# Putting two steps of a chunked scan inside an ordering block that names a matrix product

## The chip, the cores and the metric

The kernel runs on one core of one Trainium2 chip. A core has a matrix engine (PE in the profile, with its weight loads as PEld), three engines for elementwise work (DVE, ACT and POOL) and SP, which here only issues transfers. Every engine works off its own queue of instructions in the order in which they stand in it. The metric is the device time of one execution in microseconds (us).

## What is computed

One layer of a hybrid trunk over 384 rows of 2048 channels (256 rows of a new stream, and 8 running streams with 16 rows each). What matters here is the middle of it, a chunked state-space scan with 8 groups of 8 heads of 64 channels. In the reference one chunk goes so:

```python
cum = jnp.cumsum(dtc * A, axis=1)
decay = jnp.exp(jnp.where(causal, cum[:, :, None] - cum[:, None, :], -jnp.inf))
cb = jnp.einsum('btgn,bsgn->btsg', Cc, Bc)
xdt = xc * dtc[..., None]
y = jnp.einsum('btsgr,bsgrp->btgrp', cb[..., None] * decay, xdt)
y = y + jnp.einsum('btgn,bgrpn->btgrp', Cc, h) * jnp.exp(cum)[..., None]
w_end = jnp.exp(cum[:, -1][:, None] - cum)
h = h * jnp.exp(cum[:, -1])[..., None, None] + jnp.einsum('bsgn,bsgr,bsgrp->bgrpn', Bc, w_end, xdt)
```

Before it stand a normalisation and one large projection with a causal convolution, behind it a gated normalisation, two output projections and a squared-ReLU MLP. All of it is in 32-bit floats.

## The kernel before

**Large products.** Every weight tile of 128 x 1024 numbers is fetched by SP into a tile `w`, and `wsplit` (lines 66 to 72) splits it: ACT rounds it into a high part `wh` (line 70), DVE takes the difference as a low part `wl` (line 71). Three matrix products then stand for one: high by high, high by low, low by high (lines 98 to 100). PE therefore waits for ACT and DVE whenever a split is late. In the names of the profile `wl_z` is the low part of a weight tile for a z projection, `pj_z` the tile in the accumulation memory that the product goes to.

**The scan's blocks.** The loop over `g` from line 866 runs eight blocks, one for each group, and a short tail. Each block has ten projections (four for x, one each for B and C, four for z) and two pairs of heads. Between the projections stand the scan's short products, all queued on PE in a fixed row: `t_pp`, `t_cb`, `t_yT`, `t_Y`, `t_yi` and, in `state`, `t_su`. Around them lie the two steps that the change touches:

- `bside` (line 706): ACT rounds the transposed B of the block into its high part (line 708), DVE makes the low part (line 709), and nine small transfers on SP follow.
- `xside` (line 733), once for each pair: four products on DVE (line 738), two of them scaled copies `xdt` and two that scale the transposed x, `xT`, in place. Then `yis` (line 745, DVE, from the result of `t_yi`), the split of `xT` into `xhl` (lines 752 and 753), and ten small transfers on SP. `mside` follows in the first half of a block and makes `cbm` from `cb` on DVE (line 731).

The transposed x and B come from two transfers through main memory on the queue of POOL (lines 617 and 623), whose landing the steps wait for.

**What sets the order.** The kernel's functions are recorded line by line, and a scheduler of the library sets the order on each engine by what is ready first. The helper `behind` (line 56) ties the order where the kernel wants it:

```python
    def behind(ins):
        return nullcontext() if ins is None else tc.issue_after(ins.ins)
```

The library's `issue_after(ins)` adds an edge of issue order, without a wait for the end of `ins`, from each instruction that the block records *on the engine of `ins`*. Instructions of other engines in the block get none. `last[0]` is always the latest product on PE: `half`, `moving` and `lump` set it. `later` (line 75) is the other use of the helper, with `cut[0]`, a rounding on ACT, and `cut[1]`, a difference on DVE.

Of the kernel before, what the change touches and what calls it, by code (L numbers as in the profile page):

```python
# [6 lines left out]
F32 = mybir.dt.float32  # L7
F32R = mybir.dt.float32r
I32 = mybir.dt.int32
AF = mybir.ActivationFunctionType  # L10
ALU = mybir.AluOpType
# [3 lines left out]
P = 128  # L15
# [18 lines left out]
def build(ctx, tc, io):  # L34
    nc = tc.nc
    v, s, te, gp, sy = nc.vector, nc.scalar, nc.tensor, nc.gpsimd, nc.sync
# [16 lines left out]
    def sstile(name):  # L53
        return pss.tile([P, 512], F32, tag="ss", name=name)

    def behind(ins):
        return nullcontext() if ins is None else tc.issue_after(ins.ins)
# [44 lines left out]
    last = [None]  # L102
# [75 lines left out]
    def three(name):  # L178
        return [sstile(f"{name}_{b}") for b in range(3)]
# [180 lines left out]
    tok = small.tile([P, 11, NH], F32, name="tok")  # L360
    decb = small.tile([P, NH, NB], F32, name="decb")
    with tc.tile_pool(name="phc", bufs=1, reuse_waits="tile") as pc, tc.tile_pool(name="phc2", bufs=2, reuse_waits="tile") as pc2:
# [3 lines left out]
        for i in range(2):  # L366
            b = pc.tile([P, 640], F32, name=f"pbuf{i}")[:, :519]
# [190 lines left out]
    with tc.tile_pool(name="phd", bufs=2, reuse_waits="tile") as pd, tc.tile_pool(  # L558
# [5 lines left out]
        for i in range(3):  # L564
            b = pd1.tile([P, 24, 19], F32, name=f"cbuf{i}")
# [139 lines left out]

        def bside(D):
            bh, bl = (D.Bhl[:, a].rearrange("p b n -> p (b n)") for a in range(2))
            s.activation(bh, bl.bitcast(F32), AF.Copy)
            v.tensor_tensor(bl, bl.bitcast(F32), bh.bitcast(F32), ALU.subtract)
            bscr = b_scr[D.g]  # L710
            sy.dma_start(bscr, D.Bhl[:, :, 2, :].bitcast(F32))
            D.bs = bst[D.g % 2]
            for p4 in range(4):
                for h2 in range(2):
                    sy.dma_start(
                        D.bs[h2 * 64 + p4 * 16 : h2 * 64 + p4 * 16 + 16].bitcast(F32),
                        bscr.rearrange("(q h r) l n -> h l r q n", q=4, h=2)[h2, p4 // 2],
                    )
# [13 lines left out]

        def xside(S):
            S.xdt = pd.tile([P, 2, 3, P], F32, tag="xdt", name=f"xdt{S.nm}")
            for q in range(2):
                tv = S.xT[:, q].rearrange("p b (h q) -> p b h q", h=2)
                for o, i in ((S.xdt, 3), (S.xT, 6)):
                    v.tensor_tensor(
                        o[:, q].rearrange("p b (h q) -> p b h q", h=2),
                        tv,  # L740
                        tok[:, i : i + 3, S.h0 + q * 2 : S.h0 + q * 2 + 2].unsqueeze(3).to_broadcast([P, 3, 2, 64]),
                        ALU.mult,
                    )
            S.yis = pd.tile([P, 2, P], F32, tag="yis", name=f"yis{S.nm}", bufs=1)
            v.tensor_tensor(
                S.yis.rearrange("p j (h q) -> p (j h) q", h=2),
                S.yi.rearrange("p (h q) -> p h q", h=4),
                tok[:, 10, S.h0 : S.h0 + 4].unsqueeze(2).to_broadcast([P, 4, 64]),
                ALU.mult,
            )  # L750
            S.xhl = pd.tile([P, 2, 2, 3, P], F32R, tag="xhl", name=f"xhl{S.nm}", bufs=1)
            s.activation(S.xhl[:, 0], S.xT, AF.Copy)
            v.tensor_tensor(S.xhl[:, 1], S.xT, S.xhl[:, 0].bitcast(F32), ALU.subtract)
            xscr = x_scr[S.qd]
            for l in range(2):
                sy.dma_start(xscr[:, l], S.xhl[:, l, :, 2, :].bitcast(F32))
            S.xst = pd.tile([P, 4, 2 * P], F32R, tag="xst", name=f"xst{S.nm}", bufs=1)
            for p4 in range(4):
                for h2 in range(2):
                    sy.dma_start(  # L760
                        S.xst[h2 * 64 + p4 * 16 : h2 * 64 + p4 * 16 + 16].bitcast(F32),
                        xscr.rearrange("(q h r) l j n -> h l r q (j n)", q=4, h=2)[h2, p4 % 2],
                    )
# [102 lines left out]
        for g in range(G + 1):  # L866
# [37 lines left out]
            S = D.p[0]  # L904
            S.py = mmtile(f"py{S.nm}")
            if g:
                lump(lambda: t_pp(prev.p[1], S.py))
            lump(lambda: t_cb(D))
            bside(D)
            if g:  # L910
                lump(lambda: t_yT(prev.p[1]))
                lump(lambda: t_Y(prev.p[1]))
            lump(lambda: t_yi(S))
            xside(S)
            mside(D)
            if g:
# [30 lines left out]
            lump(lambda: t_Y(S))  # L947
            lump(lambda: t_yi(S1))
            xside(S1)
            state(S)  # L950
            final(S)
# [21 lines left out]
    with ExitStack() as phe:  # L973
# [21 lines left out]
        for nb in range(4):  # L995
# [4 lines left out]
            o = three(f"pj_sp{nb}")  # L1000
# [44 lines left out]
    with tc.tile_pool(name="phf", bufs=1, side="right", reuse_waits="tile") as pf, tc.tile_pool(  # L1045
# [80 lines left out]
        for nb in range(4):  # L1126
# [3 lines left out]
            o = [sstile(f"wo{nb}_{b}") for b in range(3)]  # L1130
# [156 lines left out]
    with tc.tile_pool(name="phg", bufs=1, reuse_waits="tile") as pg, tc.tile_pool(  # L1287
# [9 lines left out]
        for c8 in range(NC):  # L1297
            hh = []
            for f8 in range(8):
# [8 lines left out]
                h = pg2.tile([P, T], F32R, tag=f"hh{f8}", name=f"hh{f}", bufs=1)  # L1308
# [4 lines left out]
            for nb in range(4):  # L1313
                o = [sstile(f"wd{c8}_{nb}_{b}") for b in range(3)]
# [158 lines left out]
```

## Time and profile before

| | |
|---|---|
| median of three runs | 2702.86 us (2700.16, 2703.67, 2702.86) |
| the profiled execution | 2702.03 us |
| its span, first to last instruction | 2700.1 us |
| mean granted clock of the matrix engine | 0.993 |
| the eight blocks of the scan | from about 440 to 1220 us of the span |
| PE busy | 2647.5 us, 98% of the span |
| DVE, ACT, POOL busy | 1524.7, 1150.1, 245.2 us |

A row of waits names the engine and line that sat idle, what released it, the total in us, how often, and the longest. A row of the timeline has the start, the duration, the engine, the line, and in square brackets the idle time just ahead of it with its releaser. A row of the windows has, for each engine, the busy time and the count of instructions in that stretch, then the granted clock of PE, the share of the transfer engines and their rate.

### The profile page before, as it was taken

Reading aid. Unit: us, or ns where it says so; the run is one execution under the profiler, and the core shown is the slowest. Engines: PE = TensorE matmul, PEld = TensorE weight load, DVE = VectorE, ACT = ScalarE, POOL = GpSimd, SP = SyncE. Lnnn points to the kernel's source line nnn. Section 1 sums busy time; section 2 is a strip of 40 time slices with the busy share of each in tenths; the row PEclk is TensorE's granted clock in tenths of the full one; section 3 lists DMA queues with packets and bytes.
Section 4 is the critical chain, followed back from the end, with each engine's and each line's share of the span. In section 5 each row is a group of like instructions: output and inputs, shape, how many; then the busy total and the mean of one; then the engine's idle time right before and its main releaser. Section 6 shows DMA issues by size and latency. Waiting matters only on the chain.

```text
span 2700.1 us, 38584 instructions
## 1 busy us (share of the span) xinstructions
PE 2647.5 (98%) x15149; PEld 2463.7 (91%) x15149; DVE 1524.7 (56%) x2148; ACT 1150.1 (43%) x1806; POOL 245.2 (9%) x366
## 2 busy tenths in 40 slices
PE   9999999899999899999999999999999999999998
PEld 9998889898999899988888888989999999999897
DVE  6585336687787787866433345634444444444446
ACT  6443235456565565644422234633233333333233
POOL 0000002223223223311000000000000000000000
PEclk9999999999999999999999999999999999999999
DMA  7444446666666676766644454333334444444443
GB/s 269 152 132 157 145 151 210 201 222 224 228 228 221 207 249 209 226 205 225 230 156 156 156 187 156 125 133 135 138 133 137 137 133 136 138 133 138 135 133 132
DMA packets 153845, 467.10 MB, mean 173 GB/s; under 512 B 21120, under 2 KB 48320, under 8 KB 148672
## 3 DMA queue, kind: packets, MB, share of 16 engines
q1 hardware_dynamic: 134400, 389.90, 44.1%
q0 software_dynamic: 19264, 74.74, 8.0%
q8 instruction: 119, 1.95, 0.3%
q14 instruction: 62, 0.51, 0.1%
HBM read 414.97 MB, written 49.58 MB: 172 GB/s over the span
## 4 chain that ended last, share of the span: by engine, by line
PE 55%; DVE 2%; DMA 1%; issue 1%; ACT 0%; POOL 0%; DVEq 0%; POOLq 0%; ACTq 0%
PE pj_up L98 6%; PE pj_up L100 6%; PE pj_up L99 6%; PE wd L151 6%; PE wd L150 6%; PE wd L149 6%; PE pj_sp L149 3%; PE pj_sp L150 3%; PE pj_sp L151 3%; PE wo L151 2%; PE wo L150 2%; PE pj_gb L149 2%; PE wo L149 2%; PE pj_gb L151 2%; PE pj_gb L150 2%
## 5 line engine op out<-in xcount | busy, mean ns | idle before, releaser
L98 PE MATMUL pj_up<-x1h,wh_up 128*128 128x384 f32 (+1 forms) x1024 | 333.7, 326 | 0.0
L99 PE MATMUL pj_up<-x1l,wh_up 128*128 128x384 f32 (+1 forms) x1024 | 333.4, 326 | 0.0
L100 PE MATMUL pj_up<-x1h,wl_up 128*128 128x384 f32 (+1 forms) x1024 | 333.4, 326 | 0.0
L71 DVE TENSOR_TENSOR wl_wd<-w_wd,wh_wd 128x1024 fp32r<-128x1024 f32 x126 | 154.3, 1225 | 240.5 <-ACT wh_wd L70 240.5
L149 PE MATMUL wd<-wh_wd,hh 128*128 128x512 f32 x756 | 286.5, 379 | 0.0
L150 PE MATMUL wd<-wl_wd,hh 128*128 128x512 f32 x756 | 286.5, 379 | 0.0
L151 PE MATMUL wd<-wh_wd,hl 128*128 128x512 f32 x756 | 286.5, 379 | 0.0
L70 ACT ACTIVATE wh_wd<-w_wd 128x1024 fp32r<-128x1024 f32 x126 | 133.1, 1057 | 322.3 <-PE wd L151 261.9
L98 PE MATMUL pj_x<-xgh,wh_x 128*128 128x384 f32 x768 | 256.1, 333 | 2.6 <-DVE zs L929 2.6
L70 ACT ACTIVATE wh_up<-w_up 128x1024 fp32r<-128x1024 f32 x126 | 133.1, 1057 | 291.8 <-PE pj_up L99 231.8
L100 PE MATMUL pj_x<-xgh,wl_x 128*128 128x384 f32 x768 | 254.3, 331 | 1.0 <-DVE wl_x L71 1.0
L71 DVE TENSOR_TENSOR wl_up<-w_up,wh_up 128x1024 fp32r<-128x1024 f32 x126 | 154.3, 1225 | 177.9 <-ACT wh_up L70 177.7
L99 PE MATMUL pj_x<-xgl,wh_x 128*128 128x384 f32 x768 | 254.2, 331 | 0.0
L99 PEld LDWEIGHTS pj_up<-x1l,wh_up 128*128 128x128 f32 x1024 | 193.6, 189 | 0.2
L98 PEld LDWEIGHTS pj_up<-x1h,wh_up 128*128 128x128 f32 x1024 | 193.6, 189 | 0.2
L100 PEld LDWEIGHTS pj_up<-x1h,wl_up 128*128 128x128 f32 x1024 | 193.6, 189 | 0.0
L100 PE MATMUL pj_z<-xgh,wl_z 128*128 128x384 f32 x512 | 168.4, 329 | 12.6 <-DVE wl_z L71 12.5
L98 PE MATMUL pj_z<-xgh,wh_z 128*128 128x384 f32 x512 | 167.6, 327 | 0.8 <-ACT wh_z L70 0.8
L99 PE MATMUL pj_z<-xgl,wh_z 128*128 128x384 f32 x512 | 167.5, 327 | 0.0
L71 DVE TENSOR_TENSOR wl_sp<-w_sp,wh_sp 128x1024 fp32r<-128x1024 f32 x64 | 78.4, 1225 | 154.0 <-ACT wh_sp L70 154.0
L151 PEld LDWEIGHTS wd<-wh_wd,hl 128*128 128x128 f32 x756 | 142.9, 189 | 20.3
L149 PEld LDWEIGHTS wd<-wh_wd,hh 128*128 128x128 f32 x756 | 142.9, 189 | 20.1
(333 smaller groups left out, 5979.7 us busy)
## 6 DMA issues: line engine op xcount, KB each, us to landing
w_up<-w_up SPq DMA_DIRECT2D x128, 512.0 KB, 3.3
w_wd<-w_down SPq DMA_DIRECT2D x128, 512.0 KB, 3.3
w_x<-w_in SPq DMA_DIRECT2D x96, 512.0 KB, 4.5
w_z<-w_in SPq DMA_DIRECT2D x64, 512.0 KB, 3.9
w_sp<-w_ssd SPq DMA_DIRECT2D x64, 512.0 KB, 3.3
w_ga<-w_ga SPq DMA_DIRECT2D x32, 512.0 KB, 3.3
w_pp<-w_pp SPq DMA_DIRECT2D x32, 512.0 KB, 3.3
hs<-ssm POOLq DMA_DIRECT2D x16, 1024.0 KB, 7.1
```

The costliest lines, as they stand in the source:

```text
L70: cut[0] = s.activation(h, w, AF.Copy)
L71: cut[1] = v.tensor_tensor(l, w, h.bitcast(F32), ALU.subtract)
L98: te.matmul(out, wh, xh, start=first, stop=False, **how)
L99: te.matmul(out, wh, xl, start=False, stop=False, **how)
L100: return te.matmul(out, wl, xh, start=False, stop=last, **how)
L149: te.matmul(out, mh, vh, start=k == 0, stop=False)
L150: te.matmul(out, mh, vl, start=False, stop=False)
L151: last[0] = te.matmul(out, ml, vh, start=False, stop=k == nk - 1)
```

## The change

The four products of `xside` and the rounding of `bside` are recorded within `with behind(last[0]):`. At both places `last[0]` is a product on PE: in `bside` the last one of `t_cb`, in `xside` the last one of `t_yi`. The four products are recorded for DVE, the rounding for ACT. Nothing else is touched.

```diff
         def bside(D):
             bh, bl = (D.Bhl[:, a].rearrange("p b n -> p (b n)") for a in range(2))
-            s.activation(bh, bl.bitcast(F32), AF.Copy)
+            with behind(last[0]):
+                s.activation(bh, bl.bitcast(F32), AF.Copy)
             v.tensor_tensor(bl, bl.bitcast(F32), bh.bitcast(F32), ALU.subtract)
...
         def xside(S):
             S.xdt = pd.tile([P, 2, 3, P], F32, tag="xdt", name=f"xdt{S.nm}")
-            for q in range(2):
-                tv = S.xT[:, q].rearrange("p b (h q) -> p b h q", h=2)
-                for o, i in ((S.xdt, 3), (S.xT, 6)):
-                    v.tensor_tensor(
-                        o[:, q].rearrange("p b (h q) -> p b h q", h=2),
-                        tv,
-                        tok[:, i : i + 3, S.h0 + q * 2 : S.h0 + q * 2 + 2].unsqueeze(3).to_broadcast([P, 3, 2, 64]),
-                        ALU.mult,
-                    )
+            with behind(last[0]):
+                for q in range(2):
+                    tv = S.xT[:, q].rearrange("p b (h q) -> p b h q", h=2)
+                    for o, i in ((S.xdt, 3), (S.xT, 6)):
+                        v.tensor_tensor(
+                            o[:, q].rearrange("p b (h q) -> p b h q", h=2),
+                            tv,
+                            tok[:, i : i + 3, S.h0 + q * 2 : S.h0 + q * 2 + 2].unsqueeze(3).to_broadcast([P, 3, 2, 64]),
+                            ALU.mult,
+                        )
             S.yis = pd.tile([P, 2, P], F32, tag="yis", name=f"yis{S.nm}", bufs=1)
```

The file after has one line more from line 708 on and two more from line 736 on, so line 709 after is line 708 before, and line 740 after is line 738 before. In the built program, DVE's queue in the first block, where its second pair begins, holds these rows before (`xb` is the transposing of a tile of x, `zs` the scaling of a z projection):

```order
L612 STREAM_TRANSPOSE xb_4322<-xs_4242 128x384
L738 TENSOR_TENSOR xdt_1_4585<-xT_1_4168,tok 128x384
L738 TENSOR_TENSOR xT_1_4168<-xT_1_4168,tok 128x384
L71 TENSOR_TENSOR wl_z_1_0_4260<-w_z_1_0_4257,wh_z_1_0_4259 128x1024
L71 TENSOR_TENSOR wl_z_1_1_4294<-w_z_1_1_4291,wh_z_1_1_4293 128x1024
L929 TENSOR_TENSOR zs_0_4324<-pj_z_0_4256,rstd 128x384
```

And after:

```order
L612 STREAM_TRANSPOSE xb_4322<-xs_4242 128x384
L740 TENSOR_TENSOR xdt_1_4585<-xT_1_4168,tok 128x384
L740 TENSOR_TENSOR xT_1_4168<-xT_1_4168,tok 128x384
L71 TENSOR_TENSOR wl_z_1_0_4260<-w_z_1_0_4257,wh_z_1_0_4259 128x1024
L71 TENSOR_TENSOR wl_z_1_1_4294<-w_z_1_1_4291,wh_z_1_1_4293 128x1024
L931 TENSOR_TENSOR zs_0_4324<-pj_z_0_4256,rstd 128x384
```

No row has moved; the two scaled products stand ahead of the same two weight splits. ACT's queue around the rounding of B in the first block holds before:

```order
L70 ACTIVATE wh_z_0_0_4172<-w_z_0_0_4170 128x1024
L588 COPY cbuf_3707<-cbuf_3707 128x15x3
L589 COPY cstate<-cbuf_3707 128x27
L708 ACTIVATE Bhl_3713<-Bhl_3713 128x384
L595 ACTIVATE cacc_4161<-cbuf_3707,vec 128x384
```

And after:

```order
L70 ACTIVATE wh_z_0_0_4172<-w_z_0_0_4170 128x1024
L588 COPY cbuf_3707<-cbuf_3707 128x15x3
L589 COPY cstate<-cbuf_3707 128x27
L709 ACTIVATE Bhl_3713<-Bhl_3713 128x384
L595 ACTIVATE cacc_4161<-cbuf_3707,vec 128x384
```

Here too only the line number differs. The same holds of all five queues from first row to last, their semaphore waits included.

## The prediction

> **What bounds the kernel now.** I read the page's head first: which engine is full, and in which part of the span it isn't.
>
> ```profile
> PE 2647.5 (98%) x15149; PEld 2463.7 (91%) x15149; DVE 1524.7 (56%) x2148; ACT 1150.1 (43%) x1806; POOL 245.2 (9%) x366
> ```
>
> PE is the bound: 2647.5 of 2700.1 us, so all its idle time together is 52.6 us. The second view is the windows, cut ahead of the eight blocks of the scan, around them, and behind them.
>
> ```profile
> 0.00:440.00 440.00, 438.05 (x2291) 403.34 (x2292) 237.67 (x382) 181.54 (x261) 20.11 (x46) 1.00 0.51 174
> 440.00:1220.00 780.00, 737.90 (x5218) 708.78 (x5217) 606.85 (x877) 439.44 (x855) 212.02 (x299) 0.98 0.67 218
> 1220.00:2700.00 1480.00, 1471.56 (x7643) 1351.58 (x7641) 680.16 (x890) 529.09 (x691) 13.04 (x23) 1.00 0.45 149
> ```
>
> The first number behind the stretch's length is PE's busy time. In the blocks PE idles for 780.0 - 737.9 = 42.1 us, and in the rest of the span for 10.5. The clock granted to PE is lower there too (0.98). A change inside the blocks can win at most these 42.1 us and the little clock. The third view is the waits, for the engines that the change touches and the one that waits for them.
>
> ```profile
> DVE xdt L738 <- DMA xT<-t_scr: 69.1, 18, 6.2
> ACT Bhl L708 <- DMA Bhl<-t_scr: 19.0, 8, 5.6
> PE su L800 <- DVE cbm L731: 17.8, 6, 5.8
> DVE Bhl L709 <- ACT Bhl L708: 13.9, 8, 4.9
> PE pj_z L100 <- DVE wl_z L71: 12.5, 6, 7.1
> ```
>
> DVE stands for 69.1 us in front of the scaled copies of x, until the transposed x has landed, and ACT for 19.0 us in front of the rounding of B. PE loses 17.8 us behind the one sort of wait and 12.5 behind the other. The fourth view, the timeline at the second pair of the first block, shows how: DVE first, then PE.
>
> ```profile
> 477.96 0.58 DVE L612 STREAM_TRANSPOSE xb<-xs 128x384 f32<-128x384 f32 x1 [0.68 <-ACT xs L601]
> 484.30 0.56 DVE L738 TENSOR_TENSOR xdt<-xT,tok 128x384 f32<-128x384 f32 x1 [5.76 <-DMA xT<-t_scr]
> 484.89 0.56 DVE L738 TENSOR_TENSOR xT<-xT,tok 128x384 f32<-128x384 f32 x1
> 485.37 2.35 DVE L71 TENSOR_TENSOR wl_z<-w_z,wh_z 128x1024 fp32r<-128x1024 f32 x2
> 487.64 0.55 DVE L929 TENSOR_TENSOR zs<-pj_z,rstd 128x384 f32<-128x384 f32 x1
> ```
> ```profile
> 486.64 0.69 PE L100 MATMUL pj_z<-xgh,wl_z 128*128 128x384 f32 x1 [7.12 <-DVE wl_z L71]
> ```
>
> A scaled copy whose data is late stands at the head of DVE's queue, two weight splits stand behind it, and PE has run out of split weights: 7.12 us lost. So the target is real. What the change does to it is another question.
>
> **The change part by part.** It adds no operation and removes none. Two groups of instructions could move:
>
> ```profile
> L738 DVE TENSOR_TENSOR xdt<-xT,tok x32: 515/557/561, 446.7 to 1164.5; 128x384 f32<-128x384 f32 x32
> L738 DVE TENSOR_TENSOR xT<-xT,tok x32: 545/556/560, 447.3 to 1165.4; 128x384 f32<-128x384 f32 x32
> L708 ACT ACTIVATE Bhl<-Bhl x8: 522/522/524, 464.2 to 1127.2; 128x384 fp32r<-128x384 f32 x8
> ```
>
> *The four scaled copies of each pair.* Sixteen pairs with four copies of 0.557 us are 35.6 us of DVE. They are now recorded inside a block that names the last product of `t_yi`, which is on PE. The library ties to the named instruction only what the block records on the same engine. The block records DVE work alone, so no edge is added. The rows shown with the change bear this out: `xdt`, `xT` and two `wl_z` stand in the same places before and after. That these rows are the program that ran can be read in the timeline above, which has the same row of operations (transpose, copy, scaled x, two splits, `zs`), and DVE's 2148 instructions in the page follow the built order from first to last. Cost: 16 x 0.
>
> *The rounding of B.* Eight of 0.522 us on ACT, in a block that names the last product of `t_cb`, on PE as well: no edge, and the same place in ACT's queue. Cost: 8 x 0. Its nine transfers on SP in each block and the ten of each `xside` keep their places, and so do POOL's transfers: no queue is passed and no wait is added, so there is nothing that a lost cover could uncover.
>
> *The stalls.* The 69.1, 19.0, 17.8 and 12.5 us all stay, since nothing ahead of the waiting instructions has changed. Nothing else becomes late next.
>
> *The clock.* [...] After the 7.12 us wait the windows show it:
>
> ```profile
> 480.00:485.00 5.00, 0.00 (x0) 0.00 (x0) 0.67 (x2) 1.06 (x1) 3.20 (x5) 0.81 0.27 74
> 485.00:490.00 5.00, 3.36 (x11) 3.36 (x12) 4.32 (x5) 0.52 (x1) 0.76 (x1) 0.50 0.50 158
> 490.00:495.00 5.00, 5.00 (x32) 5.00 (x32) 2.34 (x3) 1.06 (x1) 0.00 (x0) 1.00 0.53 206
> ```
>
> With the granted clock at 0.50, 11 products take 3.36 us; at 1.00, 32 take 5.00, or 0.156 us each, so 11 would take 1.72. The wait costs 1.6 us more than its own length. [...]
>
> The sum is 0. The profiled execution took 2702.03 us, which is its span of 2700.1 and 1.9 around it, and lies 0.8 under the median of the three runs (2702.86). The four executions shown reach from 2700.16 to 2703.67 with their middle at 2702.45; I take 2702.5.
>
> **The rivals.**
>
> *The order takes hold, and it helps.* It would, if the scheduler did place the scaled copies behind work that is ready when `t_yi` is queued. Then they no longer stand at the head of DVE's queue while x is in flight, and the weight splits pass them. For it speaks that `t_yi` of the second pair comes late in its block, long after the copies at 484.30. Against it stand the rows of the order. It would give back at most the 12.5 us of PE in front of `pj_z` and the 1.6 us of slow clock behind the longest: 2702.0 - 12.5 - 1.6 = 2687.9. The 17.8 us in front of `su` would stay, for there the queue waits for B:
>
> ```profile
> 648.76 1.08 PE L661 MATMUL py<-hs,Cm 128*32 128x256 f32 x16
> ```
> ```profile
> 651.89 0.52 ACT L708 ACTIVATE Bhl<-Bhl 128x384 fp32r<-128x384 f32 x1 [5.61 <-DMA Bhl<-t_scr]
> ```
>
> The short product `t_yi` (L661) was over about 2 us before the rounding of B started, and what held the rounding was a landing; an order behind `t_cb`, which stands still further ahead, would not have held it longer. [...]
>
> *The order takes hold, and it hurts.* The copies then come right behind `t_yi`, in the first half of a block ahead of `cbm` in DVE's queue, and `cbm` (L731) is what PE's `su` already waits for. Four copies of 0.557 us in each of eight blocks are 17.8 us ahead of it. DVE's 13.9 us of idle time in front of line 709 could swallow part, which leaves 3.9. So it costs 3.9 to 17.8 us, or 2705.9 to 2719.8, with 2713 in the middle. It would decide as soon as the copies in a block take longer than DVE's pause before `cbm`, 1.7 us in the mean by 13.9 over eight, against 2.2 us of copies. For it speaks the row of `su`; against it, once more, that no row has moved.
>
> *The program is the same and the measurement isn't.* Other executions, perhaps on another chip, could put the medians over 0.2% (5.4 us) apart. That is about what a measurement of this kernel can tell from no change. The four executions shown lie 3.5 us apart, so medians of several runs should agree better than that.
>
> **How the numbers follow.** That the change doesn't do what it says is here the forecast, with 94 in 100: it rests on rows that can be read, not on an estimate. The two cases in which the order takes hold get 2 in 100 each, for a library that would build another program where the kernel is run than the one shown. The last 2 in 100 go to executions that differ by over 0.2% on their own, half to each side. Faster is then 2 + 1 = 3, slower 2 + 1 = 3, and within 0.2% the remaining 94. The range needs none of the rivals to hold 8 in 10. It reaches 4.5 us to either side of 2702.5, a little over one spread of the four executions (3.5 us): 2698.0 to 2707.0. There is no unknown cost in it, only the spread.
>
> **What the profile after would show.** If it is right: 2148 instructions on DVE, the same waits, with the scaled copies as line 740 idle for about 69 us in front of xT's landing and the rounding of B as line 709 for about 19; PE in front of `pj_z` at about 12 us and of `su` (now line 802) at about 18; in the first block, the copy still ahead of two `wl_z` and PE waiting about 7 us behind them. Waits under 3 us may differ by some tenths. It would be wrong if the copies stood behind the `wl_z` rows, with the 69.1 us gone (first rival), or if `cbm` came later and `su` waited longer (second).

## The result, and the profile after

The changed kernel takes 2702.80 us (median of twelve runs, 2694.68 to 2706.02) against 2703.88 us before (twelve runs, 2700.16 to 2707.30). The ratio is 0.9992, with a 95% interval of 0.9980 to 1.0004: no difference. The profiled execution after took 2696.29 us, 5.7 us less than that of before, though the two programs are the same; so the two profiles show how far executions of one program differ. For the experiments below: of e1's six executions one took 3966.4 us at a granted clock of 0.654, and the ratio and the time given for e1 are those of the other five (the median of all six is 2677.67 us). First the page's line of engines after, then the windows at the same cuts as before.

```profile
PE 2644.8 (98%) x15149; PEld 2460.8 (91%) x15149; DVE 1524.8 (57%) x2148; ACT 1149.8 (43%) x1806; POOL 246.3 (9%) x366
```
```profile
0.00:440.00 440.00, 437.16 (x2296) 401.99 (x2297) 237.81 (x382) 181.72 (x262) 20.27 (x46) 1.00 0.52 174
440.00:1220.00 780.00, 741.78 (x5240) 712.22 (x5240) 609.44 (x880) 441.83 (x858) 214.22 (x299) 0.98 0.68 221
1220.00:2700.00 1480.00, 1465.82 (x7617) 1346.56 (x7615) 677.55 (x887) 526.20 (x688) 11.80 (x22) 1.00 0.45 147
```

PE idles 38.2 us in the blocks, where it was 42.1, and the granted clock is 0.98 as before. The waits answer to those shown of before, with the new line numbers:

```profile
DVE xdt L740 <- DMA xT<-t_scr: 65.0, 17, 6.5
ACT Bhl L709 <- DMA Bhl<-t_scr: 19.7, 8, 5.6
PE su L802 <- DVE cbm L732: 17.3, 6, 6.0
DVE Bhl L710 <- ACT Bhl L709: 14.6, 8, 4.9
PE pj_z L100 <- DVE wl_z L71: 14.9, 7, 4.8
```

Every wait is still there and hangs on the same releaser. At the second pair of the first block the timeline shows DVE's row unchanged, and then PE:

```profile
477.58 0.58 DVE L612 STREAM_TRANSPOSE xb<-xs 128x384 f32<-128x384 f32 x1 [0.68 <-ACT xs L601]
482.39 0.56 DVE L740 TENSOR_TENSOR xdt<-xT,tok 128x384 f32<-128x384 f32 x1 [4.23 <-DMA xT<-t_scr]
482.98 0.56 DVE L740 TENSOR_TENSOR xT<-xT,tok 128x384 f32<-128x384 f32 x1
483.46 2.35 DVE L71 TENSOR_TENSOR wl_z<-w_z,wh_z 128x1024 fp32r<-128x1024 f32 x2
485.73 0.55 DVE L931 TENSOR_TENSOR zs<-pj_z,rstd 128x384 f32<-128x384 f32 x1
```
```profile
484.73 0.43 PE L100 MATMUL pj_z<-xgh,wl_z 128*128 128x384 f32 x1 [4.81 <-DVE wl_z L71]
```

The copy still stands ahead of the two splits and waits for its landing, this time 4.23 us and not 5.76, and PE loses 4.81 us and not 7.12. The order is the program's: in both profiles the instructions of each engine stand in the same row from first to last (15149 products on PE, 2148, 1806 and 366 instructions on DVE, ACT and POOL, 984 transfers on SP). How long each wait is belongs to the execution. The product that the block names for these copies, the last one of the second pair's `t_yi`, runs only here:

```profile
512.33 1.08 PE L661 MATMUL py<-hs,Cm 128*32 128x256 f32 x16
```

The copies started from 482.39 us on, some 30 us ahead of it. So no order behind that product holds on the chip.

### The profile page after: what moved, and what is told of

It reads as the page before. It is cut to its first block, busy times and chain, and to the rows that moved or that the text cites. A ratio compares the mean times of both kernels' runs of the same rounds, so it can differ in the third digit from the quotient of the medians.

```text
span 2694.4 us, 38584 instructions
## 1 busy us (share of the span) xinstructions
PE 2644.8 (98%) x15149; PEld 2460.8 (91%) x15149; DVE 1524.8 (57%) x2148; ACT 1149.8 (43%) x1806; POOL 246.3 (9%) x366
## 4 chain that ended last, share of the span: by engine, by line
PE 57%; DVE 1%; DMA 0%; ACT 0%; issue 0%; POOL 0%; DVEq 0%; POOLq 0%; ACTq 0%
PE pj_up L98 6%; PE pj_up L99 6%; PE pj_up L100 6%; PE wd L151 6%; PE wd L149 6%; PE wd L150 6%; PE pj_sp L149 3%; PE pj_sp L151 3%; PE pj_sp L150 3%; PE pj_gb L149 2%; PE pj_gb L150 2%; PE pj_gb L151 2%; PE wo L150 2%; PE wo L149 2%; PE wo L151 2%; PE pj_z L100 0%
## 5 line engine op out<-in xcount | busy, mean ns | idle before, releaser
L100 PE MATMUL pj_z<-xgh,wl_z 128*128 128x384 f32 x512 | 168.4, 329 | 14.9 <-DVE wl_z L71 14.9
```

The lines of the kernel that those rows point to most:

```text
L100: return te.matmul(out, wl, xh, start=False, stop=last, **how)
```

## The experiments

The theory: the change does nothing because its blocks name a product on PE, while the instructions in them belong to DVE and ACT. If so, the same idea with an instruction of the right engine should move the time. The first rival: such a wait on DVE is hidden, and even a real order moves nothing. The second: a real order hurts. All edits are told against the kernel before, and each ratio is to that kernel on the same chip. e9 and e10 ran on another chip than e1 to e8; the kernel before took 2700.90 us there (seven runs), so across the two, compare ratios and not times.

### The copies behind a weight split (e1)

```diff
         def xside(S):
...
-            for q in range(2):
+            with later():
+                for q in range(2):
...
```

`later` names the latest weight split of each engine, so the four copies now follow an instruction on DVE.

> The four scaled copies of each pair are tied behind the latest weight split on DVE (an instruction of their own engine) instead of a product on PE. Theory: the change did nothing because the named instruction was on another engine; with an edge that exists, the copies leave the head of DVE's queue. Then DVE's idle time in front of them falls from 65 to 69 us to under 15, PE's wait in front of pj_z from 12.5 to 14.9 us to under 4, the wait in front of su stays at 17 to 18, and the kernel takes 2688 to 2695 us. Rival: DVE's wait hides behind other work and PE's waits only change their place: within 0.2% of before. Second rival: the copies now stand in front of cbm, su waits longer, and the kernel takes 2706 us or more.

Measured: 2676.33 us, ratio 0.9899 (0.9881 to 0.9917), 27 us faster. First PE's waits. Of DVE's waits around the blocks, the row of 65 to 69 us in front of the copies is gone; the first two are now these, the second of them in front of B's low part:

```profile
PE su L801 <- DVE cbm L731: 18.7, 7, 4.8
PE pj_x L98 <- DVE cbuf L581: 2.5, 1, 2.5
PE cb L652 <- ACT xs L601: 1.3, 1, 1.3
```
```profile
DVE wl_x L71 <- ACT wh_x L70: 41.4, 56, 5.9
DVE Bhl L709 <- ACT Bhl L708: 26.6, 8, 6.0
```

No wait in front of `pj_z` is left. The theory holds in its waits, and both rivals fall. Its time doesn't: it gave 2688 to 2695 us, and the gain is about twice the 12.5 us of the wait that went.

### The words of the change, done on DVE (e2)

```diff
         def xside(S):
             S.xdt = pd.tile([P, 2, 3, P], F32, tag="xdt", name=f"xdt{S.nm}")
+            S.yis = pd.tile([P, 2, P], F32, tag="yis", name=f"yis{S.nm}", bufs=1)
+            yi = v.tensor_tensor(
...
+            with behind(yi):
+                for q in range(2):
...
```

`yis` reads the result of `t_yi`, so what follows it on DVE truly stands behind the short products.

> The words of the change done on DVE: yis, which needs the result of the last short product, comes first, and the four copies are tied behind it. Theory: as in the run with the copies behind a split, the wait of DVE for xT is gone and pj_z waits under 4 us, but 2.2 us of copies for each pair now stand ahead of the additions that follow su; 2688 to 2700 us. Rival that hurts: these 2.2 us, sixteen times, fall on PE: 2706 to 2738 us. Rival without effect: within 0.2%.

Measured: 2676.71 us, ratio 0.9900 (0.9885 to 0.9915), the same as e1 within the intervals and again below the time that the theory gave. `pj_z` has no wait of note, and `su` waits 13.5 us:

```profile
PE su L801 <- DVE cbm L731: 13.5, 7, 2.9
PE cb L652 <- ACT xs L601: 1.3, 1, 1.3
PE pj_gb L149 <- DVE hs L810: 1.3, 1, 1.3
```

So the idea behind the change, done for the copies, was worth 1%. What it lacked was an edge.

### Which pair's copies (e5 and e6)

The edit of e1 with `later() if S.jp == 1 else nullcontext()` (e5, the second pair of each block) and `S.jp == 0` (e6, the first).

> Only the second pair's copies are tied behind the latest weight split. Theory: the waits in front of pj_z come from these copies, which stood right ahead of wl_z; so pj_z waits under 4 us, su still 13 to 19 us, and the run gets most of what tying all copies got (2677.67 us): 2675 to 2688 us. Rival: the gain came from the first pair, whose copies stood ahead of the weight splits of x: then 2698 us or more here.

Measured: 2675.85 us, ratio 0.9907 (0.9889 to 0.9925). `pj_z` waits 0.7 us, `su` 16.6:

```profile
PE su L801 <- DVE cbm L731: 16.6, 6, 5.5
PE pj_z L100 <- DVE wl_z L71: 0.7, 1, 0.7
```

> Only the first pair's copies are tied. Theory: the waits in front of pj_z stay (12 to 17 us) and the kernel takes 2695 to 2707 us. Rival: 2690 us or less, and the second pair's run shows little.

Measured: 2704.63 us, ratio 1.0005 (0.9993 to 1.0016).

```profile
PE su L801 <- DVE cbm L731: 26.1, 7, 8.3
PE pj_z L100 <- DVE wl_z L71: 8.9, 5, 3.6
```

The waits in front of `pj_z` fell to 8.9 us, which I had not expected, but those in front of `su` rose to 26.1. The gain of e1 is that of the second pair alone, whose copies stood right ahead of the z splits. Tying the first pair as well adds nothing that can be measured.

### The step of B (e3 and e7)

In e3 the step is recorded later and tied behind the latest split of each engine:

```diff
             lump(lambda: t_cb(D))
-            bside(D)
...
             zproj(0)
+            with later():
+                bside(D)
             pload(D.p[1])
```

> The whole step of B (rounding on ACT, low part on DVE, nine transfers) is recorded behind the first z projection and tied behind the latest weight split of each engine; the copies stay as before. Theory: PE's 17.3 to 17.8 us in front of su come from the rounding's wait for its landing, which holds cbm up on DVE; they fall under 5 us, the copies' wait of 65 to 69 us stays, and the kernel takes 2682 to 2690 us. Rival: cbm is late for another reason (wl_z or xhl ahead of it in DVE's queue): su still waits over 10 us and the time is within 0.2%.

Measured: 2702.49 us, ratio 0.9994 (0.9986 to 1.0002). PE's waits, then the first of DVE's:

```profile
PE pj_z L100 <- DVE wl_z L71: 16.4, 8, 4.2
PE cb L652 <- ACT xs L601: 9.5, 7, 2.5
PE pj_x L100 <- DVE wl_x L71: 6.6, 7, 1.6
PE su L800 <- DVE cbm L731: 4.8, 6, 0.8
PE pj_x L98 <- DVE zs L928: 4.8, 5, 1.4
```
```profile
DVE xdt L738 <- DMA xT<-t_scr: 91.4, 24, 6.9
```

The cause of the wait in front of `su` was right: it fell from 17.8 to 4.8 us. The time was wrong, for the theory gave 2682 to 2690 us: the gain was handed on. DVE now stands 91.4 us in front of the copies of x, 22 more than before, and PE loses the time in smaller pieces elsewhere. In e7 the rounding stays and `cbm` alone is put ahead of B's low part:

```diff
             lump(lambda: t_cb(D))
+            mside(D)
             bside(D)
...
             s.activation(bh, bl.bitcast(F32), AF.Copy)
-            v.tensor_tensor(bl, bl.bitcast(F32), bh.bitcast(F32), ALU.subtract)
+            with behind(D.cut):
+                v.tensor_tensor(bl, bl.bitcast(F32), bh.bitcast(F32), ALU.subtract)
...
             xside(S)
-            mside(D)
```

> cbm is recorded ahead of the step of B and B's low part is tied behind it on DVE; the rounding stays where it is on ACT, the copies as before. Theory of a stall handed on: su waits under 6 us, as in the run with the whole step of B later, but PE then reaches the second pair sooner against a landing that comes no sooner, the copies' wait for xT rises over 75 us, pj_z takes up the loss, and the kernel takes 2698 to 2707 us. Rival: the run with the later step of B gained nothing because the later step cost something of its own (its transfers, or the rounding between splits); then 2680 to 2690 us here.

Measured: 2702.10 us, ratio 1.0002 (0.9988 to 1.0017). The time is as the theory says, two of its numbers aren't: `su` still waits 13.5 us, and the copies' wait is 60.8 us and no larger; but `pj_z` waits 22.3 us.

```profile
PE pj_z L100 <- DVE wl_z L71: 22.3, 8, 6.6
PE su L801 <- DVE cbm L732: 13.5, 6, 5.3
```
```profile
DVE xdt L739 <- DMA xT<-t_scr: 60.8, 22, 5.2
```

So e7 is a weak test, since it took only 4.3 us off `su`'s wait. Neither edit gains anything while the copies stand in front of the splits.

### Both (e4), and one of the two in another form (e10)

e4 joins the edits of e1 and e3.

> Copies behind the latest weight split, and the step of B behind the first z projection. Theory: the two waits are separate, so the gains add: PE idles 10 to 15 us in the eight blocks instead of 38 to 42, and the kernel takes 2668 to 2680 us. Rival: one stall hides the other, and the gain is no more than the larger of the two.

Measured: 2647.59 us, ratio 0.9799 (0.9787 to 0.9812), 56 us faster, where e1 alone gave 27 and e3 alone 1. The theory's 2668 to 2680 us was too slow and its rival is out. The window of the blocks, and PE's waits:

```profile
440.00:1220.00 780.00, 776.36 (x5474) 745.36 (x5473) 640.49 (x919) 462.39 (x885) 216.63 (x307) 1.00 0.72 233
```
```profile
PE pj_x L98 <- DVE cbuf L581: 2.5, 1, 2.5
PE warm_o L238 <- DVE warm L234: 1.2, 1, 1.2
PE su L801 <- DVE cbm L731: 0.6, 2, 0.4
```

PE idles 3.6 us of these 780. The gains don't add, they depend on each other: as long as the copies wait at the head of DVE's queue, time won earlier in the block is lost there (91.4 us of waiting in e3). With that gone, the wait of B is worth its full length and the slow clock behind it (granted clock in the blocks 0.98 in e1, 1.00 in e4): from e1's profile to that of e4, PE's idle time fell by 19.7 us (33.9 to 14.2) and its busy time by 17.3 (2648.4 to 2631.1). The profiled execution of e1 is the slowest of its five (2684.41 us), so the second number is on the large side.

e10 joins e1 with e7.

> Copies behind the latest weight split, and cbm ahead of B's low part on DVE; B's rounding keeps its place on ACT. Theory: with the copies' wait gone, the wait in front of su is worth its length and the slow clock behind it: su waits under 6 us, and the kernel takes 2650 to 2665 us. Rival: the rounding's wait on ACT holds wh_z up whether cbm is early or not, and PE's loss shows in front of pj_z: 2668 to 2680 us.

Measured: 2664.27 us, ratio 0.9857 (0.9837 to 0.9878), between e1 and e4: about 11 us better than e1 by the ratios. The time lies within the theory's range, the wait of `su` doesn't: it is still 8.9 us. The rounding keeps its place on ACT and waits there 33.5 us; with the whole step moved, in e4, `su` waits 0.6 us.

```profile
PE su L802 <- DVE cbm L732: 8.9, 4, 3.0
```
```profile
ACT Bhl L708 <- DMA Bhl<-t_scr: 33.5, 8, 6.8
```

### The copies behind the short products with a later step of B (e8 and e9)

e8 joins e2 with e3; e9 is the same with the step of B behind `zproj(1)` in place of `zproj(0)`.

> Copies behind yis, the words of the change, with the step of B behind the first z projection. Theory: it doesn't matter which instruction of DVE the copies follow, if it stands behind the weight splits that PE needs next; 2645 to 2652 us, as with the copies behind a split (2647.59 us). Rival: the copies ahead of su's additions cost something that the wait for cbm had hidden: 2653 to 2665 us.

Measured: 2695.13 us, ratio 0.9984 (0.9973 to 0.9996). Theory and rival both miss: most of the 27 us that e2 had won are gone again. PE's waits show the old place, and SP's queue in one block (its rows are marked SPq) a likely cause:

```profile
PE pj_z L100 <- DVE wl_z L71: 30.1, 15, 4.9
PE pj_z L98 <- ACT wh_z L70: 3.8, 4, 1.8
```
```profile
662.63 0.52 SPq L711 DMA_DIRECT2D b_scr<-Bhl  x1
663.20 1.13 SPq L63 DMA_DIRECT2D w_z<-w_in  x2
666.70 3.65 SPq L715 DMA_DIRECT2D bst<-b_scr  x8
670.39 0.91 SPq L63 DMA_DIRECT2D w_z<-w_in  x2
```

The first transfer of B is issued at 662.63, when its low part has been made, and the fetches of four weight tiles of z stand behind it, two of them also behind the eight small ones. ACT then waits for those fetches (first row, against the second in e9 below), DVE for ACT, PE for DVE. The sum of ACT's wait alone doesn't decide it, for in e2 it is 27.1 us without a wait in front of `pj_z`.

```profile
ACT wh_z L70 <- DMA w_z<-w_in: 39.1, 26, 5.1
```
```profile
ACT wh_z L70 <- DMA w_z<-w_in: 11.8, 11, 1.9
```

> Copies behind yis as in the run that took 2695.13 us, but the step of B is recorded behind the second z projection instead of the first, which puts its first transfer behind four weight fetches on SP's queue that stood behind it there. Theory: in that run SP stood in front of b_scr until B's low part was made, the weights of z behind it came late, and wl_z with them; now wl_z is on time, pj_z waits under 6 us and the kernel takes 2645 to 2660 us. Rival: DVE is simply too full behind yis (copies, xhl and the additions of su in one burst), and the place of the transfers changes nothing: 2685 us or more.

Measured: 2646.20 us, ratio 0.9792 (0.9777 to 0.9807). Only the place of B's step differs from e8, and by the ratios about 52 us go with it. PE's longest wait is now this one:

```profile
PE pj_gb L149 <- DVE hs L810: 1.3, 1, 1.3
```

The waits of SP in front of B's first transfer, in e8 and then in e9:

```profile
SPq L711 <- DVE Bhl L709: 30.6, 7, 4.8
```
```profile
SPq L711 <- DVE Bhl L709: 2.4, 1, 2.4
```

That B's step as a whole is what matters is shown; that it is its transfers on SP and not its two instructions on ACT and DVE is what the queue shows, and no run moved the transfers alone. It fits that e4, with B's step recorded at the same place as in e8, has one fetch of z behind the first transfer around 660 us where e8 has four, and that SP waits in front of these transfers for 11.8 us in all and not 30.6. e9 and e4 beat both kernels, and their ratios can't be told from each other.

## Why the prediction was right, step by step

*No edge, so nothing moves.* Right. The time is the same within the interval, and the rows of waits and of the timeline stand as named, down to the line numbers. e1 and e2 show that the copies can be moved: tied to an instruction of DVE, they gave 27 us. These two edits also name an instruction at another place; that the engine is what matters rests on the library's rule, on the queues, and on the copies that ran 30 us ahead of the product named. That the forecast 2702.5 and the measured 2702.80 us lie 0.3 us apart is luck: four medians of the kernel before, over different sets of runs, go from 2700.90 to 2703.88.

*The stalls.* That all of them stay is right: 65.0, 19.7, 17.3 and 14.9 us after, against 69.1, 19.0, 17.8 and 12.5. PE's single waits differed by more than the last part of the prediction says: it named about 7 us in the first block, where 4.81 were measured, 2.3 less than before.

*The rival that helps, priced at 2687.9 us.* Its mechanism is right, and `su`'s wait stayed about as it said (13.5 us in e2, 16.6 in e5). Its price was too small: e2 gained 27 us, not 14.1. Two terms were mis-sized. The larger is PE's idle time, which I capped at the 12.5 us in front of `pj_z`; the other is the slow clock, which I counted behind the longest wait alone (1.6 us). In e5, whose profiled execution lies next to its median, the span fell by 26.9 us from 2700.1 to 2673.2. PE's idle time fell by 21.0 of these (52.6 to 31.6) and its busy time by 5.9 (2647.5 to 2641.6). Besides the wait in front of `pj_z`, small ones had gone, such as those of `pj_gb` (3.0 us) and `pj_x` (2.6). How much of that belongs to the execution is open: the profile after, of the same program as before, has 49.6 us of idle time.

The slow clock counts for more where nearly all waits go, as in e4. There the span fell by 54.8 us from 2700.1 to 2645.3. PE's idle time fell by 38.4 of these (52.6 to 14.2), and the other 16.4 are PE's busy time, 2647.5 to 2631.1 for the same 15149 products, with the granted clock in the blocks at 1.00 in place of 0.98. The clock record of the trace has 30.7 us at 0.50 within the blocks before and 27.3 after; in e4 and e9 the windows give the blocks 1.00. PE is busy for 24.0 of the 30.7 us. At 0.305 us a product in the stretch at 0.50 behind the wait of 7.12 us (11 in 3.36 us) and 0.156 at 1.00, these 24.0 us have lost about 11.7, an estimate; where the rest of the 16.4 comes from is open. The slow clock can follow short waits too. In the kernel before, behind a wait of 2.11 us:

```profile
843.77 0.48 PE L800 MATMUL su<-xst,bst 64*128 64x256 f32 x3 [2.11 <-DVE cbm L731]
```
```profile
840.00:845.00 5.00, 2.89 (x41) 2.07 (x30) 4.97 (x9) 4.14 (x7) 0.00 (x0) 1.00 0.77 251
845.00:848.00 3.00, 3.00 (x11) 3.00 (x10) 3.00 (x7) 2.67 (x9) 1.54 (x2) 0.50 0.33 87
```

So here 2.11 us without a product, just behind the scan's short products, were followed by a stretch at 0.50. The clock record has three such stretches of 3.41 us in the blocks (from 844.95, 943.94 and 1131.67 us) and three of 6.83 us (from 483.14, 653.81 and 749.38). Not every such wait is followed so: of the seven waits from 2.04 to 3.31 us in these blocks, the four in front of `su` are, while 2.62 us at 891, 2.06 at 1061 and 3.05 at 1178 us aren't; and in the profile after, waits of 3.02 and 2.25 us in front of `su` aren't either. What decides it is open.

*The rival that hurts.* It put the copies ahead of `cbm`. Done on DVE (e2), the scheduler put them behind `cbm`, and nothing was lost. In e1 they stand between B's low part and `cbm`, much as the rival had it (around 650 us they start at 648.52, `cbm` at 652.05): `su` waits 18.7 us, hardly more than the 17.8 before, and the kernel is still 27 us faster. What did hurt was on another queue: in e8 a step of B that had been put among the weight fetches held SP up (30.6 us in front of B's first transfers, 2.4 in e9).

*The spread.* The range of 4.5 us to either side was drawn from four executions 3.5 us apart. The median lies in it, but twelve runs after span 11.3 us, and three of them lie below 2698.0. The cases for a median were right, the spread of single executions was taken too small.

## What to carry to other kernels

An order that is asked for is worth what it does to the queues: read the order of the built program first, and where nothing has moved, look at which engine the named instruction belongs to. An instruction that waits for a transfer should stand behind whatever on its engine feeds the bound engine next: in e1 that was worth 27 us. Transfers on an issuing queue are worth the same look: in e8 a small store that waits for a result (30.6 us over the blocks) stands on SP in front of four weight fetches, though no run moved the transfers alone. Stalls of one chain hide each other: here a single removal showed nothing (e3, ratio 0.9994) or half (e1, 0.9899), and both together more than their sum (e4, 0.9799).

## What was not expected of the hardware

PE's waits cost more than their length: 38.4 us less idle time in e4 came with 16.4 us less busy time for the same products, and 21.0 us in e5 with 5.9. The half clock behind a wait of 2.11 us was not expected either: the prediction counted it behind the wait of 7.12 us alone. Whether the spread goes with the waits isn't shown. Runs of the kernel before and after lie within 7.1 and 11.3 us, those of e4 within 5.3 (five runs, 2646.87 to 2652.17) and of e9 within 3.1 (four runs, 2645.12 to 2648.19); but the four runs of e5, whose granted clock in the blocks is still 0.99, lie within 2.9 (2674.39 to 2677.26).
